# A two-block decoder layer stack in split float32: the second block's products with activations as the stationary operand

## The chip, the cores and the metric

One core of one Trainium2 chip runs the whole program. The metric is the device time of one execution in microseconds (us), lower is better. Engines by the names of the profile: PE is the matrix engine (its weight loads are PEld), DVE the vector engine, ACT the scalar engine, POOL the general one, SP the queue that issues the weight transfers. A matmul on PE holds a block of 128 x 128 numbers in the array (the stationary operand, brought in by a weight load) and streams up to 512 columns past it (the moving operand); the result goes to PSUM, eight banks of 128 x 512 numbers.

## The reference, cut to what matters

256 tokens, 2048 features, all in float32. A first block (a pooling layer and a sparse attention layer, each under a modulated norm) gives `x`; the change is in the second block alone:

```python
def second_block(x, p, ...):
    h = rmsnorm(x, attn_norm_g)
    u, v_sgu, q, k, v_att, g_a, g_b = split(h @ w_in)        # 1024 x 5, 2048 x 2 columns
    ...                                                       # y_a from u, v_sgu; y_b from q, k, v_att
    q, k = rmsnorm(q per head, q_norm_g), rmsnorm(k per head, k_norm_g)      # 8 heads of 128
    merged = sigmoid(g_a) * (y_a @ w_up_a) + sigmoid(g_b) * (y_b @ w_up_b)
    x = x + merged @ w_o
    h = rmsnorm(x, ffn_norm_g)
    gate, up = split(h @ w_ffn_in)                            # 2 x 5632 columns
    x = x + (silu(gate) * up) @ w_ffn_out
    return x + sigmoid(rmsnorm(x, ple_norm_g) @ w_ple_gate) * (p @ w_ple)
```

## The kernel before, in words

Every float32 operand of a large product is split in two numbers of a shorter kind, a high part and a low part (the rest), and a product is three: high x high, high x low, low x high. Weights come from HBM in pieces of 512 rows x 512 columns (1 MB), at most `RAWB = 8` under way. ACT casts half a piece (256 rows) to its high part (`split_half`, L1633), DVE subtracts it to get the low part (`late_low`, L1623); this runs up to `SPLB = 5` half pieces ahead of the products. All of this lies in 20 slots of 8 KB per partition (`F`), handed out by hand, and a slot that a product has read goes to a later split.

A `Group` is a product with 512 columns of a weight, over row tiles of 128 ("row tile" below means 128 rows of one group's 512 columns). `mm_half` (L1690 on) issues it half a piece at a time, and its `orient` says which operand is stationary:

- orient A (weights stationary, features on partitions in the output). Per row tile and each of the four blocks of 128 output features: one matmul of the high weights with the high and low activations side by side (512 columns, L1715) and one of the low weights with the high activations (256 columns, L1719). The output needs four banks, and each bank's two halves are summed in the eviction (`evsum`: ACT copies one, L391, DVE adds, L393).
- orient B (activations stationary, tokens on partitions in the output). Per row tile and each of the two blocks of 128 tokens: three matmuls of 512 columns (L1724 to L1726: high activations with high weights, the same with low weights, low activations with high weights). The output needs two banks.

The order of the work is written out by hand: `seq` lists the pieces, and the loop at the end of the program goes through the halves: splits ahead (`prepare`), products (`mm_half`), and in between it steps generators. Evictions (`evac`, `evq`) are stepped after the products of every output block (`pump_ev`) and after every half; side tasks (`task`, `side`) once per half (`pump`). A generator's `yield` puts off what follows by one step, and `lag(n)` by n; so the place of an eviction's instructions in each engine's queue is set by the number of yields, and the engines run their queues in order. Evictions and tasks share PSUM with the products (from the attention on, `PM` may hold 5 banks and `PA`, the tasks', 3), and small tiles come from slots too (`H` six of 4 KB, `W` three of 2 KB, `E` nine of 1 KB).

Stages, with names of the code: `P1` pool, `P2` attention, `P3` the second block's mixers (groups q0, k0, v0, v1, q1, k1, two of the gating's v, two of its u, then four times g_a, g_b, up_a, up_b, then four of w_o), `P4` the feed-forward part (6 pairs of gate and up groups, four of w_ffn_out over those 6 blocks, then 5 pairs and four more), `P5` the per-layer embedding. Before the change v, the gating's v and P5 are of orient B, the rest of P3 and P4 of orient A. The evictions that matter: `ev_b2qk` and the task `qknorm` (squares on ACT, sums over a head's features by PE with `ones` L1186, the factors spread over partitions by PE L1202, the product on DVE L1205); `ev_sig`, `ev_upa`, `ev_upb`; `ev_residual` (w_o and w_ffn_out); `ev_fgate`, `ev_fup`; `start_b2` (the second block's norm: it makes `Rn` and `En` per token from a PE product, L1118, and then scales the residual in 16 DVE instructions, L1130); `start_ffn` and `start_ple` (norms); `x_natural` (the residual turned to tokens on partitions, 8 times 4 PE transposes, L1468). `split` and `split_scaled` make the operand of the next product from a result with features on partitions.

Of the kernel before, what the change touches and what calls it, by code (L numbers as in the profile page):

```python
# [19 lines left out]
T = 256            # tokens  # L20
# [28 lines left out]
class Slots:  # L49
    """Slots of one size on chip, handed out by hand; the longest free one goes first."""  # L50
# [37 lines left out]
class Share:  # L88
    """A user of slots that others use as well, with no more than cap of them."""
# [19 lines left out]
class Part:  # L109
    """Some of the columns of a slot; the slot is free when all its parts are."""  # L110
# [11 lines left out]
class Op:  # L122
    """An operand with features on partitions: per feature tile the high and low parts, 256 tokens each."""
# [27 lines left out]
class Op32:  # L151
    """An operand with features on partitions, as it is: n feature tiles in a slot."""
# [42 lines left out]
class ModPiece:  # L195
    """Rows and columns of a modulation weight: 128 k x 512 n times (4, 1) or (2, 2)."""
# [12 lines left out]
def model_kernel(ctx: ExitStack, tc: tile.TileContext, A, out):  # L209
# [27 lines left out]
    # ---------------------------------------------------------------- tasks beside the main line of products  # L237
# [38 lines left out]
    def lag(n=2):  # L276
        """Before a product in a task: time for the other engines to get its operands ready."""
# [5 lines left out]
    def last_of(key, n=4):  # L283
        """True for the last of the n output tiles that get here."""
# [6 lines left out]
    def take(where, key, nt, shape=(128, 4, T)):  # L291
        """For the output tiles of a group: its slot, asked for by the first one."""
# [4 lines left out]
    # ---------------------------------------------------------------- constants and small vectors  # L297
# [15 lines left out]
    def rows(i, what):  # L313
        """Vectors as rows of 128, turned into columns."""
# [58 lines left out]

    def split_scaled(op, kt, v, g):
        """v * g (per feature) into operand tile kt."""
# [6 lines left out]
    def evsum(ps, dst=None):  # L382
        """A product in PSUM, its two halves summed if it has two."""
# [16 lines left out]
    class Sum:  # L400
        """Sum of squares over features, per token (still spread over partitions)."""

        def __init__(self, tail=0):
            self.n = self.started = 0
            # the last ones stay apart, for PE to add
# [21 lines left out]
        def total(self, n=3):  # L427
            """Sums per token, on all partitions."""
# [30 lines left out]
    sums = {k: Sum() for k in ("x0", "x2", "x2g", "x3", "x4")}  # L459
# [62 lines left out]
    # ---------------------------------------------------------------- modulation  # L522
# [10 lines left out]
    def mod_work(p, half):  # L533
# [3 lines left out]
        if p.kk + half == 0:  # L537
            # while heads are at work the smaller slots are taken
# [22 lines left out]
    def mod_fin(key, wide, wait):  # L561
        """Sums over partitions, plus the bias; the gain of the norm; the operand that becomes ready."""
# [26 lines left out]
    # ---------------------------------------------------------------- phase 1: pool  # L589
# [4 lines left out]
    def pool_consts():  # L594
        """The pooling over tokens as matrices [s, t], less the identity: tokens 0-127 to all, 128-255 to their own."""
# [124 lines left out]
    # ---------------------------------------------------------------- phase 2: sparse attention  # L720
# [13 lines left out]
    def rope_tables():  # L734
        """cos and signed sin: for heads of 128 (partitions 0-31), of 64 (all partitions), and with
        tokens on partitions for the index keys."""
# [20 lines left out]
        # sign of the sine: minus for the first half of a head's turned features  # L757
# [36 lines left out]
        def reduced(dst, ang, shift):  # L794
            """ang + shift * 2 pi, brought to [-pi, pi]."""
# [37 lines left out]
    # index keys and weights: the last 128 columns (48 of the index queries, 64 keys, 16 weights)  # L833
# [100 lines left out]
    def topk_task():  # L934
        """0 for the keys that a query attends to, a large negative number for the others."""
# [62 lines left out]
    def head_attn(g, j):  # L998
# [25 lines left out]
        # columns: keys 0 of queries 0 and 1, keys 1 of queries 1  # L1024
# [73 lines left out]
    # ---------------------------------------------------------------- phase 3: second block, its mixers  # L1098
# [24 lines left out]
        # eps / R^2, for the norms of q and k  # L1123
# [4 lines left out]
        # the residual that the second block starts from  # L1128
# [6 lines left out]
    def b2_consts():  # L1135
        # stick-breaking looks at strictly earlier keys; partition: key, column: query
# [5 lines left out]
        # [j', j]: 1 where j' >= j  # L1142
# [18 lines left out]
        for g in range(8):  # L1161
            # partition: s, column: t; keep t >= s
# [5 lines left out]
    def ev_b2qk(name, n):  # L1168
        def ev(nt, ps):
            yield from take(blk, (name, n), nt)  # L1170
            yield from evsum(ps, blk[name, n].t[:, nt, :])
            if last_of((name, n)):
                task(qknorm(name, n))
        return ev

    def qknorm(name, n):
        x = blk[name, n].t
        g = vcol("q_norm_g") if name == "q" else kgs
        ss = yield from PA.new([128, 2, 4])
        for j0 in (0, 2):  # L1180
            q = yield from W.new([128, 2, T])
            S.activation(q.t, x[:, j0:j0 + 2, :], AF.Square)
            yield from lag()
            for j in range(2):
                for tt in range(2):
                    PE.matmul(ss.t[:, tt, j0 + j:j0 + j + 1], q.t[:, j, cols(tt)], ones[:, 0:1], start=True, stop=True)  # L1186
            q.free()
        yield from until(lambda: "En" in blk)
        yield
        r = small((128, 2, 4))  # L1190
        V.scalar_tensor_tensor(r, ss.t, 1.0 / 128.0, blk["En"][:, :, None].to_broadcast([128, 2, 4]), op0=ALU.mult,
                               op1=ALU.add)
        ss.free()
        S.activation(r, r, AF.Sqrt)
        V.reciprocal(r, r)
        yield from lag()
        for j0 in (0, 2):
            # each token's factor, on all partitions
# [595 lines left out]
```

## Time and profile before

| | |
|---|---|
| device time, median of 3 runs | 2427.67 us (2427.65 to 2427.88) |
| the profiled execution, first to last instruction (span) | 2425.4 us; no other time of it is given |
| PE busy / weight loads busy | 2382.0 us (98%) / 2089.2 us (86%) |
| DVE / ACT / POOL busy | 1675.9 us (69%) / 1209.2 us (50%) / 121.9 us (5%) |
| matmuls on PE | 13855 |
| DMA | 522.82 MB, mean 216 GB/s |

The profiled execution's own time is known as its span; the median of the runs is 2.3 us more, which is what lies around the first and the last instruction. Busy time of an engine is the union of its instructions' records. Records of matmuls overlap (the next one starts before the record of the one ahead has ended), so a mean duration of a matmul is not its share of the time; the step from one start to the next is read from the timeline. A row of a group of instructions gives line, engine, operation, tiles (written <- read), shapes, count, busy time and mean duration in ns, then the engine's idle time before them and who ended it.

### The profile page before, as it was taken

Reading aid. Unit: us, or ns where it says so; the run is one execution under the profiler, and the core shown is the slowest. Engines: PE = TensorE matmul, PEld = TensorE weight load, DVE = VectorE, ACT = ScalarE, POOL = GpSimd, SP = SyncE. Lnnn points to the kernel's source line nnn. Section 1 sums busy time; section 2 is a strip of 40 time slices with the busy share of each in tenths; the row PEclk is TensorE's granted clock in tenths of the full one; section 3 lists DMA queues with packets and bytes.
Section 4 is the critical chain, followed back from the end, with each engine's and each line's share of the span. In section 5 each row is a group of like instructions: output and inputs, shape, how many; then the busy total and the mean of one; then the engine's idle time right before and its main releaser. Section 6 shows DMA issues by size and latency. Waiting matters only on the chain.

```text
span 2425.4 us, 34213 instructions
## 1 busy us (share of the span) xinstructions
PE 2382.0 (98%) x13855; PEld 2089.2 (86%) x13855; DVE 1675.9 (69%) x2396; ACT 1209.2 (50%) x1777; POOL 121.9 (5%) x218
## 2 busy tenths in 40 slices
PE   5999999999999999999999999999999999999999
PEld 5899998988888888888888888888888888888887
DVE  7987899776978887654575667666565456656564
ACT  3444435444465566454754545555444445445553
POOL 0200084000100000000000000000000000000000
PEclk8999999999999999999999999999999999999999
DMA  9988998845556677444455557455455575456372
GB/s 366 387 299 325 332 341 331 313 157 173 174 187 231 227 276 244 156 139 149 149 187 177 184 168 276 155 195 171 159 185 162 190 248 195 149 181 216 123 244 104
DMA packets 246930, 522.82 MB, mean 216 GB/s; under 512 B 8362, under 2 KB 10644, under 8 KB 246516
## 3 DMA queue, kind: packets, MB, share of 16 engines
q1 hardware_dynamic: 246324, 519.20, 61.9%
q8 instruction: 108, 1.77, 0.3%
q0 software_dynamic: 448, 1.44, 0.2%
q14 instruction: 50, 0.41, 0.0%
HBM read 518.51 MB, written 2.10 MB: 215 GB/s over the span
## 4 chain that ended last, share of the span: by engine, by line
PE 92%; DVE 5%; ACT 1%; issue 1%; DMA 1%; POOL 0%; SPq 0%; DVEq 0%; ACTq 0%; POOLq 0%
PE bank L1715 42%; PE bank L1719 21%; PE bank L1724 5%; PE bank L1726 5%; PE bank L1725 5%; PE bank L1709 3%; PE bank L1712 3%; PE bank L1711 3%; DVE f L1623 2%; DVE h L554 2%; PE bank L1705 1%; PE bank L570 1%; PE bank L472 0%; PE bank L1202 0%; PE bank L639 0%
## 5 line engine op out<-in xcount | busy, mean ns | idle before, releaser
L1715 PE MATMUL bank<-f,f 128*128 128x512 f32 x4432 | 1556.0, 400 | 0.0
L1623 DVE TENSOR_TENSOR f<-f,f 128x1024 fp32r<-128x1024 f32 x788 | 945.9, 1218 | 378.6 <-ACT f L1633 377.9
L1719 PE MATMUL bank<-f,f 128*128 128x256 f32 x4432 | 1196.1, 280 | 0.0
L1633 ACT CAST f<-f 128x1024 fp32r<-128x1024 f32 x788 | 800.3, 1041 | 573.8 <-PE bank L1719 257.7
L1715 PEld LDWEIGHTS bank<-f,f 128*128 128x128 f32 x4432 | 814.0, 188 | 177.0
L1719 PEld LDWEIGHTS bank<-f,f 128*128 128x128 f32 x4432 | 836.3, 189 | 25.7
L393 DVE TENSOR_TENSOR e<-bank,e 128x256 f32<-128x256 f32 x240 | 101.3, 423 | 206.7 <-ACT e L391 205.9
L1709 PE MATMUL bank<-f,f 128*128 128x256 f32 x768 | 221.5, 288 | 0.0
L1711 PE MATMUL bank<-f,f 128*128 128x256 f32 x768 | 218.9, 285 | 0.0
L1712 PE MATMUL bank<-f,f 128*128 128x256 f32 x768 | 218.8, 285 | 0.0
L1724 PE MATMUL bank<-f,f 128*128 128x512 f32 x528 | 211.0, 400 | 4.7 <-ACT f L511 4.7
L391 ACT COPY e<-bank 128x256 f32<-128x256 f32 x281 | 102.7, 370 | 219.2 <-PE bank L1715 217.8
L1726 PE MATMUL bank<-f,f 128*128 128x512 f32 x528 | 207.3, 393 | 1.1 <-DVE f L513 1.1
L1725 PE MATMUL bank<-f,f 128*128 128x512 f32 x528 | 206.7, 391 | 0.0
L554 DVE SCALAR_TENSOR_TENSOR h<-f,csil,h 128x512 f32<-128x512 f32 (+1 forms) x202 | 195.5, 1003 | 2.3 <-DMA f<-in_mod_w_dram 0.5
L1709 PEld LDWEIGHTS bank<-f,f 128*128 128x128 f32 x768 | 149.0, 194 | 2.8 <-issue 2.3
L1711 PEld LDWEIGHTS bank<-f,f 128*128 128x128 f32 x768 | 149.0, 194 | 0.3
L1712 PEld LDWEIGHTS bank<-f,f 128*128 128x128 f32 x768 | 148.9, 194 | 0.0
L1724 PEld LDWEIGHTS bank<-f,f 128*128 128x128 f32 x528 | 100.0, 189 | 27.2 <-ACT f L511 4.8
L1726 PEld LDWEIGHTS bank<-f,f 128*128 128x128 f32 x528 | 99.7, 189 | 24.1 <-DVE f L513 2.3
L1725 PEld LDWEIGHTS bank<-f,f 128*128 128x128 f32 x528 | 100.1, 190 | 19.6
L369 ACT CAST f<-e 128x256 fp32r<-128x256 f32 x100 | 40.4, 406 | 78.4 <-DVE e L1434 29.5
(286 smaller groups left out, 1342.6 us busy)
## 6 DMA issues: line engine op xcount, KB each, us to landing
f<-in_mod_w_dram SPq DMA_DIRECT2D x96, 1024.0 KB, 8.0
f<-in_w_ffn_in_dram SPq DMA_DIRECT2D x88, 1024.0 KB, 5.1
f<-in_attn_w_in_dram SPq DMA_DIRECT2D x72, 1024.0 KB, 5.5
f<-in_w_in_dram SPq DMA_DIRECT2D x72, 1024.0 KB, 5.2
f<-in_w_ffn_out_dram SPq DMA_DIRECT2D x44, 1024.0 KB, 5.1
f<-in_pool_w_in_dram SPq DMA_DIRECT2D x32, 1024.0 KB, 10.3
f<-in_pool_w_out_dram SPq DMA_DIRECT2D x16, 1024.0 KB, 8.2
f<-in_attn_w_out_dram SPq DMA_DIRECT2D x16, 1024.0 KB, 5.5
```

Of the source, the lines that this page charges most:

```text
L391: S.copy(a.t, ps.t[:, T:2 * T])
L554: V.scalar_tensor_tensor(acc, p.slot.t[:, k, :], c, acc, op0=ALU.mult, op1=ALU.add)
L1623: V.tensor_sub(ll, r, hh)
L1633: S.copy(hh[:, :, :nw], r)
L1709: PE.matmul(o, hh[:, i, cols(t)], op.h(kt), start=beg and t % 2 == 0, stop=False, skip_group_check=True)
L1711: PE.matmul(o, hh[:, i, cols(t)], op.l(kt), start=False, stop=False, skip_group_check=True)
L1712: PE.matmul(o, ll[:, i, cols(t)], op.h(kt), start=False, stop=end, skip_group_check=True)
L1715: PE.matmul(b, hh[:, i, cols(t)], op.x(kt), start=beg, stop=end, skip_group_check=True)
L1719: PE.matmul(b[:, 0:T], ll[:, i, cols(t)], op.h(kt), start=False, stop=False, skip_group_check=True)
L1724: PE.matmul(b, xh, hh[:, i, :], start=beg, stop=False, skip_group_check=True)
L1725: PE.matmul(b, xh, ll[:, i, :], start=False, stop=False, skip_group_check=True)
L1726: PE.matmul(b, xl, hh[:, i, :], start=False, stop=end, skip_group_check=True)
```

## The change

Groups q and k (4), g_a and g_b (8), up_a and up_b (8), all of w_ffn_in (22) and w_ffn_out (8) become orient B. Their outputs then have tokens on partitions, so:

- factors per token become per-partition scalars of the activation itself (`ev_sig`, `ev_fgate`, `ev_fup`), and evictions read PSUM directly, 512 columns at a time, without `evsum`;
- what is the operand of a next product is turned back to features on partitions by PE transposes, four of 128 x 128 per 512 columns and token block: new helper `turned` (for `merged` and `act`), in `ev_b2qk` (for q and k), and `h4_task` (for the last gate's operand);
- the norm of q and k is done per token on ACT and DVE (`qknorm` with its PE products is gone);
- the residual is turned to tokens on partitions at the start of the feed-forward part (in `start_ffn`; `x_natural` at its end is gone), w_ffn_out adds to that (`ev_ffn_out`), and the last norm's sums of squares come from ACT's accumulator instead of DVE and PE.

The groups of w_o and of the gating's u stay orient A. Comments are removed too, so line numbers of the changed file differ.

```diff
+TL = 3
...
+    def turned(op, b, tt, a):
+        yield from lag(TL)
+        ps = yield from PA.new([128, 4, 128])
+        for j in range(4):
+            PE.transpose(ps.t[:, j, :], a.t[:, cols(j)], ident)
+        a.free()
+        yield
+        yield from op.room(4 * b)
+        op.x(4 * b)
+        t = op.s[b].t
+        hi, lo = t[:, :, cols(tt)], t[:, :, T + tt * 128:T + tt * 128 + 128]
+        S.copy(hi, ps.t)
+        yield
+        V.tensor_sub(lo, ps.t, hi.bitcast(F32))
+        ps.free()
+        if last_of((id(op), b), 2):
+            op.done.update(range(4 * b, 4 * b + 4))
...
     def ev_b2qk(name, n):
...
+        def ev(tt, ps):
+            yield from take(blk, (name, n), tt)
+            a = yield from W.new()
+            S.activation(a.t, ps.t, AF.Square)
+            yield from until(lambda: "En" in blk)
+            yield
+            r = small((128, 4))
+            V.tensor_reduce(r, heads(a.t), axis=AX.X, op=ALU.add)
+            V.tensor_scalar(r, r, 1.0 / 128.0, blk["En"][:, tt:tt + 1], op0=ALU.mult, op1=ALU.add)
+            yield
+            S.activation(r, r, AF.Sqrt)
+            yield
+            V.reciprocal(r, r)
+            V.tensor_mul(heads(a.t), heads(ps.t), r[:, :, None].to_broadcast([128, 4, 128]))
+            ps.free()
+            yield from lag(TL)
+            ps = yield from PA.new([128, 4, 128])
+            for j in range(4):
+                PE.transpose(ps.t[:, j, :], a.t[:, cols(j)], ident)
+            a.free()
+            yield
+            S.activation(blk[name, n].t[:, :, cols(tt)], ps.t, AF.Identity, scale=g)
...
-    def qknorm(name, n):
...
     def ev_sig(name):
-            a = yield from evsum(ps)
-            V.tensor_mul(a.t, a.t, blk["R"].t)
-            yield
-            S.activation(blk[name].t[:, nt, :], a.t, AF.Sigmoid)
+            S.activation(blk[name].t[:, tt, :], ps.t, AF.Sigmoid, scale=blk["Rn"][:, tt:tt + 1])
...
     def ev_upb(n):
+            a = yield from W.new()
+            V.tensor_mul(a.t, ps.t, blk["gb"].t[:, tt, :])
+            ps.free()
+            V.tensor_add(a.t, a.t, blk["ga"].t[:, tt, :])
...
+            yield from turned(merged, n, tt, a)
...
     def start_ffn():
...
+        ps = yield from PA.new([128, 2])
+        for tt in range(2):
+            PE.matmul(ps.t[:, tt:tt + 1], s.s.t[:, cols(tt)], ones[:, 0:1], start=True, stop=True)
...
+        for n in range(4):
+            for tt in range(2):
+                ps = yield from PA.new()
+                for j in range(4):
+                    PE.transpose(ps.t[:, cols(j)], xt(n * 4 + j)[:, cols(tt)], ident)
+                yield
+                S.copy(ple["x"][tt].t[:, cols(n, 512)], ps.t)
...
     def ev_fup(g):
+            a = yield from W.new()
+            V.scalar_tensor_tensor(a.t, ps.t, ffn["R"][:, tt:tt + 1], ffn["g"].t[:, tt, :], op0=ALU.mult, op1=ALU.mult)
+            ps.free()
...
+            yield from turned(act, g, tt, a)
...
+    def ev_ffn_out(n, last):
+        def ev(tt, ps):
+            yield from until(lambda: ple["xn"] > n)
+            x = ple["x"][tt].t[:, cols(n, 512)]
+            V.tensor_add(x, ps.t, x)
+            ps.free()
+            if last:
+                yield
+                q = yield from W.new()
+                S.activation(q.t, x, AF.Square, accum_out=ssq[:, tt, n:n + 1])
...
+    def h4_task(n):
+        yield from lag(TL)
+        for k in (0, 2):
+            ps = yield from PA.new([128, 2, T])
+            for j in range(2):
+                for tt in range(2):
+                    PE.transpose(ps.t[:, j, cols(tt)], ple["x"][tt].t[:, cols(n * 4 + k + j)], ident)
+            evac(h4_split(n * 4 + k, ps))
+            yield
...
-        P3.append(Group(W_in2, n0, h2, ALLK, ev_b2qk(name, n),
+        P3.append(Group(W_in2, n0, h2, ALLK, ev_b2qk(name, n), orient="B",
...
-            P4.append(Group(W_fi, HID + g * 512, h3, ALLK, ev_fup(g), fin=h3.free if g == 10 else None))
+            P4.append(Group(W_fi, HID + g * 512, h3, ALLK, ev_fup(g), orient="B", fin=h3.free if g == 10 else None))
...
-            P4.append(Group(W_fo, n * 512, act, range(c0, c1), ev_residual(n, h4 if lastc else None, "ple_norm_g", "x4"),
-                            fin=fin if n == 3 else None))
+            P4.append(Group(W_fo, n * 512, act, range(c0, c1), ev_ffn_out(n, lastc), orient="B",
+                            pre=(lambda: preload(AF.Sqrt)) if lastc and n == 3 else None, fin=fin if n == 3 else None))
```

Three places of the two programs' instruction lists follow; in them lines of the old program are those of the profile, and of the new one L1138 is the old L1118 (the product that gives `Rn`), L1176 the old L1156 (constants), L1664 the old L1623 (low parts of weights), L1150 the old L1130, L1765 to L1767 the old L1724 to L1726; L1213 and L380 are transposes, and the new L1202 is the sum over a head on DVE. A line of "..." leaves out rows of matmuls that only continue a bank.

PE at the start of P3, before: q0 and k0 are of orient A, and the norm's small products stand between the matmuls of v0 (`bank_252`, `bank_253`).

```order
L1118 MATMUL bank_251_9158<-ident_69,e_168_9083 128x1 x2
...
L1156 MATMUL bank_256_9283<-ident_69,h_47_8853 128x128 x4
L1202 MATMUL bank_257_9288<-ident_69,small_9228 128x128 x4
L1724 MATMUL bank_252_9235<-f_590_9161,f_538_8335 128x512
...
L1202 MATMUL bank_258_9318<-ident_69,small_9228 128x128 x4
L1186 MATMUL bank_255_9258<-ones_70,w_63_9259 128x1 x4
```

The same place now (`bank_243` and `bank_244` are k0's, `bank_247` and `bank_250` v0's, `w_61` to `w_63` the normed q0 and k0).

```order
L1138 MATMUL bank_246_9093<-ident_69,e_164_9042 128x1 x2
L1765 MATMUL bank_243_8974<-f_585_9025,f_564_8772 128x512
...
L1765 MATMUL bank_247_9129<-f_587_9044,f_524_8119 128x512
...
L1176 MATMUL bank_248_9149<-ident_69,h_47_8843 128x128 x4
L1176 MATMUL bank_249_9162<-ident_69,h_47_8843 128x128 x4
L1765 MATMUL bank_250_9186<-f_587_9044,f_524_8119 128x512
...
L1765 MATMUL bank_247_9129<-f_588_9061,f_524_8119 128x512
...
L1213 MATMUL bank_251_9202<-ident_69,w_63_9105 128x128 x4
L1213 MATMUL bank_252_9207<-ident_69,w_62_8966 128x128 x4
L1213 MATMUL bank_253_9212<-ident_69,w_61_8958 128x128 x4
```

Between the product for `Rn` and the first transposes of q and k stand 30 matmuls of 512 columns (12 of k0, 18 of v0) and 8 transposes of constants; three batches of transposes then follow each other.

DVE at the same place now, from the copy of `Rn` to the last of the three products that those transposes read.

```order
L1141 COPY Rn_9116<-bank_246_9093 128x2
...
L1150 SCALAR_TENSOR_TENSOR f_3_102<-f_3_102,cols_5_76,e_162_8931 128x256 x4
L1664 TENSOR_TENSOR f_593_9126<-f_577_8929,f_593_9126 128x1024
L1202 TENSOR_REDUCE small_9136<-w_63_9105 128x4
...
L1150 SCALAR_TENSOR_TENSOR f_3_102<-f_3_102,cols_5_76,e_162_8931 128x256 x4
L1150 SCALAR_TENSOR_TENSOR f_4_103<-f_4_103,cols_5_76,e_162_8931 128x256 x4
L1207 RECIPROCAL small_9136<-small_9136 128x4
L1208 TENSOR_TENSOR w_63_9105<-bank_243_8974,small_9136 128x512
...
L1208 TENSOR_TENSOR w_61_8958<-bank_240_8794,small_9142 128x512
```

Twelve of the sixteen scalings of the residual, one subtraction for the weights, three sums over heads and the three products stand ahead of the last batch.

DVE where the first up group of P4 ends, before (four banks, `bank_406` to `bank_409`; L393 sums a bank's halves, L1432 and L1434 are the factors, L371 the low part for the next product).

```order
L1623 TENSOR_TENSOR f_918_14285<-f_899_14013,f_918_14285 128x1024
L393 TENSOR_TENSOR e_298_14310<-bank_406_14161,e_298_14310 128x256
L393 TENSOR_TENSOR e_299_14317<-bank_407_14168,e_299_14317 128x256
L1432 TENSOR_TENSOR e_298_14310<-e_298_14310,e_293_14076 128x256
L393 TENSOR_TENSOR e_300_14325<-bank_408_14174,e_300_14325 128x256
...
L1434 TENSOR_TENSOR e_298_14310<-e_298_14310,h_71_14125 128x256
L1623 TENSOR_TENSOR f_919_14304<-f_899_14013,f_919_14304 128x1024
...
L371 TENSOR_TENSOR f_921_14342<-e_298_14310,f_921_14342 128x256
```

DVE where an up group ends now (`bank_384` and `bank_385` hold it; L389 is the low part, from the transposes' banks).

```order
L1664 TENSOR_TENSOR f_944_13712<-f_931_13577,f_944_13712 128x1024
L1463 SCALAR_TENSOR_TENSOR w_79_13735<-bank_384_13617,R_88_13220,h_72_13602 128x512
L1463 SCALAR_TENSOR_TENSOR w_80_13743<-bank_385_13624,R_88_13220,h_72_13602 128x512
L1664 TENSOR_TENSOR f_945_13727<-f_931_13577,f_945_13727 128x1024
L1664 TENSOR_TENSOR f_947_13748<-f_934_13612,f_947_13748 128x1024
L389 TENSOR_TENSOR f_948_13775<-bank_387_13758,f_948_13775 128x4x128
```

PE at the same place now (`bank_386` and `bank_388` are the next group's).

```order
L1767 MATMUL bank_384_13617<-f_939_13663,f_892_13099 128x512
L1765 MATMUL bank_385_13624<-f_939_13663,f_892_13099 128x512
...
L1765 MATMUL bank_386_13751<-f_941_13680,f_856_12503 128x512
...
L380 MATMUL bank_387_13758<-ident_69,w_79_13735 128x128 x4
L1765 MATMUL bank_388_13763<-f_941_13680,f_856_12503 128x512
```

One DVE instruction per token block stands where there were sixteen per group, and the transposes of a token block stand 12 matmuls of 512 columns behind the last matmul of its bank.

## Rows read from the trace of the kernel before

**Rows 1.** The page: busy time by engine, granted clock in 40 slices.

```profile
PE 2382.0 (98%) x13855; PEld 2089.2 (86%) x13855; DVE 1675.9 (69%) x2396; ACT 1209.2 (50%) x1777; POOL 121.9 (5%) x218
PEclk8999999999999999999999999999999999999999
```

**Rows 2.** Waits of PE from 915 us to the end: total, times, longest.

```profile
PE bank L1262 <- ACT h L1257: 0.9, 1, 0.9
```

**Rows 3.** Groups of instructions by shape, PE: orient A, the norm's products, transposes.

```profile
L1715 PE MATMUL bank<-f,f 128*128 128x512 f32 x4432 | 1556.0, 400 | 0.0
L1719 PE MATMUL bank<-f,f 128*128 128x256 f32 x4432 | 1196.1, 280 | 0.0
L1202 PE MATMUL bank<-ident,small 128*128 128x128 f32 x64 | 8.4, 274 | 0.0
L1186 PE MATMUL bank<-ones,w 128*128 128x1 f32 x64 | 7.6, 239 | 0.0
L1468 PE MATMUL bank<-ident,f 128*128 128x128 f32 x32 | 4.8, 272 | 0.0
```

**Rows 4.** Timeline of PE in P4, orient A: start, record, engine, line.

```profile
1699.84 0.40 PE L1715 MATMUL bank<-f,f 128*128 128x512 f32 x1
1700.07 0.28 PE L1719 MATMUL bank<-f,f 128*128 128x256 f32 x1
...
1705.49 0.40 PE L1715 MATMUL bank<-f,f 128*128 128x512 f32 x1
```

**Rows 5.** Timeline of PE in P5, orient B.

```profile
2345.01 0.39 PE L1726 MATMUL bank<-f,f 128*128 128x512 f32 x1
2345.24 0.39 PE L1724 MATMUL bank<-f,f 128*128 128x512 f32 x1
...
2351.81 0.39 PE L1726 MATMUL bank<-f,f 128*128 128x512 f32 x1
```

**Rows 6.** Windows: stretch, PE, PEld, DVE, ACT, POOL busy (count), granted clock, DMA share, GB/s.

```profile
1640.00:1840.00 200.00, 200.00 (x1136) 173.61 (x1135) 120.67 (x175) 97.63 (x141) 0.00 (x0) 1.00 0.52 169
2340.00:2380.00 40.00, 40.00 (x178) 33.11 (x177) 24.86 (x27) 19.25 (x21) 0.00 (x0) 1.00 0.53 180
```

**Rows 7.** Timeline of PE in P5: orient B, and one batch of four transposes in it.

```profile
2332.22 0.40 PE L1725 MATMUL bank<-f,f 128*128 128x512 f32 x1
...
2334.53 0.39 PE L1726 MATMUL bank<-f,f 128*128 128x512 f32 x1
2334.77 0.60 PE L1468 MATMUL bank<-ident,f 128*128 128x128 f32 x4
...
2335.43 0.40 PE L1725 MATMUL bank<-f,f 128*128 128x512 f32 x1
```

**Rows 8.** Timeline of PE in P3: one batch of the norm's small products.

```profile
1024.44 0.39 PE L1726 MATMUL bank<-f,f 128*128 128x512 f32 x1
1024.67 1.05 PE L1202 MATMUL bank<-ident,small 128*128 128x128 f32 x8
...
1025.79 0.39 PE L1725 MATMUL bank<-f,f 128*128 128x512 f32 x1
```

**Rows 9.** Timeline at the start of P3: PE's product for Rn, then DVE.

```profile
992.28 0.50 PE L1118 MATMUL bank<-ident,e 128*128 128x1 f32 x4
...
992.82 0.16 DVE L1121 COPY Rn<-bank 128x2 f32<-128x2 f32 x1 [1.71 <-PE bank L1118]
993.49 1.67 DVE L1130 SCALAR_TENSOR_TENSOR f<-f,cols,e 128x256 f32<-128x256 f32 x4
```

**Rows 10.** Groups by shape, DVE and ACT, from 915 us to the end: prices of evictions.

```profile
L1623 DVE TENSOR_TENSOR f<-f,f 128x1024 fp32r<-128x1024 f32 x517 | 622.6, 1222 | 338.6 <-ACT f L1633 338.1
L1518 DVE TENSOR_TENSOR w<-w,h 128x512 f32<-128x512 f32 x8 | 5.5, 689 | 32.1 <-ACT w L1515 32.1
L1294 DVE TENSOR_REDUCE sguss<-h 128x8 f32<-128x1024 f32 x2 | 2.4, 1212 | 0.0
```

**Rows 11.** Timeline of DVE around the end of an up group in P4.

```profile
1706.80 0.42 DVE L393 TENSOR_TENSOR e<-bank,e 128x256 f32<-128x256 f32 x1 [4.45 <-ACT e L391]
```

More of the change, by code (lines that the diff above doesn't have):

```diff
@@ L457, in xt @@
         return res[kt // 8].t[:, kt % 8, :]
-    sums = {k: Sum() for k in ("x0", "x2", "x2g", "x3", "x4")}
+    sums = {k: Sum() for k in ("x0", "x2", "x2g", "x3")}
     sums["x1"] = Sum(TAIL)
@@ L1168, in ev_b2qk @@
     def ev_b2qk(name, n):
[L1169 to L1173, printed above, removed]
-        return ev
-    def qknorm(name, n):
[L1177 to L1188, printed above, removed]
-        yield
[L1190 to L1197, printed above, removed]
-            ps = yield from PA.new([128, 2, T])
-            for j in range(2):
-                for tt in range(2):
-                    PE.matmul(ps.t[:, j, cols(tt)], r[:, tt, j0 + j:j0 + j + 1].to_broadcast([128, 128]), ident,
-                              start=True, stop=True)
-            yield
-            V.scalar_tensor_tensor(x[:, j0:j0 + 2, :], x[:, j0:j0 + 2, :], g, ps.t, op0=ALU.mult, op1=ALU.mult)
-            ps.free()
-        yield from lag()
-        blk["normed", name, n] = True
@@ new lines, in ev_b2qk, with heads @@
+        g = vcol("q_norm_g") if name == "q" else kgs
+        def heads(t):
+            return t.rearrange("p (h d) -> p h d", h=4)
+        def ev(tt, ps):
[21 more added lines that the diff above has]
+            ps.free()
+            yield from lag()
+            if last_of((name, n), 2):
+                blk["normed", name, n] = True
@@ L1413, in model_kernel @@
     ffn = {}
+    ple = {"xn": 0}
     def start_ffn():
-        ps = yield from sums["x3"].total()
-        blk["R"].free()
-        ffn["R"] = yield from rstd(ps)
-    def ev_fgate(nt, ps):
-        yield from take(ffn, "g", nt)
-        a = yield from evsum(ps)
-        yield from until(lambda: "R" in ffn)
-        V.tensor_mul(a.t, a.t, ffn["R"].t)
-        yield
-        S.activation(ffn["g"].t[:, nt, :], a.t, AF.Silu)
-        a.free()
-    def ev_fup(g):
-        def ev(nt, ps):
-            a = yield from evsum(ps)
-            V.tensor_mul(a.t, a.t, ffn["R"].t)
-            yield
-            V.tensor_mul(a.t, a.t, ffn["g"].t[:, nt, :])
-            yield
-            yield from split(act, g * 4 + nt, a.t)
-            a.free()
-            if last_of("fup"):
-                ffn.pop("g").free()
-        return ev
+        s = sums["x3"]
+        yield from until(lambda: s.n == KT)
+        yield from lag()
+        ps = yield from PA.new([128, 2])
+        for tt in range(2):
+            PE.matmul(ps.t[:, tt:tt + 1], s.s.t[:, cols(tt)], ones[:, 0:1], start=True, stop=True)
+        s.s.free()
+        blk["R"].free()
+        yield
+        r = tl(const, [128, 2], "R3")
+        S.activation(r, ps.t, AF.Sqrt, scale=1.0 / D, bias=epsc)
+        ps.free()
+        yield
+        V.reciprocal(r, r)
+        ffn["R"] = r
+        yield from F.room(2)
+        ple["x"] = [F.get() for _ in range(2)]
+        for n in range(4):
[3 more added lines that the diff above has]
+                    PE.transpose(ps.t[:, cols(j)], xt(n * 4 + j)[:, cols(tt)], ident)
+                yield
+                S.copy(ple["x"][tt].t[:, cols(n, 512)], ps.t)
+                ps.free()
+            ple["xn"] += 1
+            if n % 2:
+                res[n // 2].free()
@@ new lines, in h4_task, with h4_split @@
+    def h4_task(n):
[6 more added lines that the diff above has]
+            evac(h4_split(n * 4 + k, ps))
+            yield
+    def h4_split(kt, ps):
+        yield
+        for j in range(2):
+            yield from split_scaled(h4, kt + j, ps.t[:, j, :], vcol("ple_norm_g", kt + j, 1))
+        ps.free()
@@ L1451, in fin @@
                     act.free(b)
-            P4.append(Group(W_fo, n * 512, act, range(c0, c1), ev_residual(n, h4 if lastc else None, "ple_norm_g", "x4"),
-                            fin=fin if n == 3 else None))
+            P4.append(Group(W_fo, n * 512, act, range(c0, c1), ev_ffn_out(n, lastc), orient="B",
+                            pre=(lambda: preload(AF.Sqrt)) if lastc and n == 3 else None, fin=fin if n == 3 else None))
     pT = Op(F)
-    ple = {"xn": 0}
-    def x_natural(n):
-        yield from lag(3)
-        if n == 0:
-            yield from F.room(2)
-            ple["x"] = [F.get() for _ in range(2)]
-        yield from until(lambda: "x" in ple)
-        for tt in range(2):
-            ps = yield from PA.new()
-            for j in range(4):
-                PE.transpose(ps.t[:, cols(j)], xt(n * 4 + j)[:, cols(tt)], ident)
-            yield
-            S.copy(ple["x"][tt].t[:, cols(n, 512)], ps.t)
-            ps.free()
-        ple["xn"] += 1
     def p_task():
@@ L1488, in start_ple @@
     def start_ple():
-        s = sums["x4"]
-        yield from until(lambda: s.n == KT)
-        yield from lag()
-        ps = yield from PA.new([128, 2])
-        for tt in range(2):
-            PE.matmul(ps.t[:, tt:tt + 1], s.s.t[:, cols(tt)], ones[:, 0:1], start=True, stop=True)
-        s.s.free()
+        r = tl(const, [128, 2], "Rp")
         yield
-        r = tl(const, [128, 2], "Rp")
-        S.activation(r, ps.t, AF.Sqrt, scale=1.0 / D, bias=epsc)
-        ps.free()
+        V.tensor_reduce(r, ssq, axis=AX.X, op=ALU.add)
+        yield
+        S.activation(r, r, AF.Sqrt, scale=1.0 / D, bias=epsc)
         yield
@@ L1512, in ev @@
         def ev(tt, ps):
-            yield from until(lambda: "R" in ple and ple["xn"] > n)
+            yield from until(lambda: "R" in ple)
             s = yield from W.new()
@@ L1527, in model_kernel @@
     for n in range(4):
-        P5.append(Group(A["w_ple_2"][0], n * 512, pT, [0], ev_ple(n), orient="B", nk=2,
-                        pre=(lambda: task(start_ple())) if n == 0 else None))
+        P5.append(Group(A["w_ple_2"][0], n * 512, pT, [0], ev_ple(n), orient="B", nk=2))
         P5.append(Group(A["w_ple_gate_2"][0], n * 512, h4, ALLK, ev_pgate(n), orient="B"))
```

57 lines of the change are left out of this document (33 added, 24 removed).

## The prediction

> **What bounds the kernel now.** I read the page first, then PE's waits, then the stages' windows and timelines. PE is busy for 98% of the span, and its granted clock stands at the upper of its two levels, 2.4 GHz, from the second fortieth on [rows 1]. From 915 us, where the second block starts, to the end, PE waits for others 0.9 us in all [rows 2]. In a stretch of the feed-forward part PE is full, DVE has 120.67 of 200 us, ACT 97.63, DMA a share of 0.52 [rows 6]. So in the stages that the change touches the time is the sum of PE's steps, and faster evictions are worth nothing by themselves. What counts: how long PE needs for the same products in the other orient, what PE work comes in and goes, and whether PE is made to wait.
>
> **The trap in the durations.** The records of matmuls are 400 ns (512 columns) and 280 ns (256) [rows 3]. Added up they give 4 x 680 = 2720 ns for a row tile of orient A, and about 6 x 395 = 2370 ns for orient B. But the records overlap: starts follow each other by 0.23 and 0.12 us [rows 4]. I use steps from start to start alone.
>
> **What each part costs on PE.**
>
> Orient A: 16 pairs of a 512-column and a 256-column matmul take 1705.49 - 1699.84 = 5.65 us, 0.353 us a pair [rows 4]; 1136 instructions in 200 us give 0.352 [rows 6]. A row tile has four pairs: 1.410 us. Orient B: 30 matmuls take 2351.81 - 2345.01 = 6.80 us, 0.2267 each [rows 5]; the window of 40 us with 178 agrees to 1%, as its count takes in those cut at the edges [rows 6]. A row tile has six: 1.360 us. Both have 3072 columns per row tile; B has six matmuls and weight loads, A eight.
>
> Row tiles that change: q and k 4 x 16 = 64, g_a and g_b 8 x 16 = 128, up_a and up_b 8 x 8 = 64, w_ffn_in 22 x 16 = 352, w_ffn_out 4 x 44 = 176; 784 of the 4432 / 4 = 1108 of orient A [rows 3]. Saved: 784 x 0.050 = **39.2 us**.
>
> Transposes added: 8 batches of four for q and k, 8 for `merged`, 22 for `act`, 8 for the last gate's operand: 46. The residual's 8 batches only move from the end of the feed-forward part to its start. One batch between matmuls of orient B: from 2334.53 to 2335.43 there are 0.90 us for two matmuls and the batch, so 0.90 - 0.45 = 0.445 us [rows 7]. Added: 46 x 0.445 = **20.5 us**.
>
> Gone: the small products of `qknorm`, 64 instructions at L1202 and 64 at L1186 [rows 3], 16 batches of eight. One costs 1025.79 - 1024.44 - 2 x 0.227 = 0.90 us [rows 8]; I price the L1186 batches alike. Removed: **14.4 us**. The small products of the two later norms come out even within half a microsecond.
>
> Added waits. (1) The start of P3, the place shown in the lists. The norm of q0 and k0 must wait for `En`. Counted from the start of the product for `Rn`, DVE's copy comes at 0.54 us and the first four scalings end at 2.9 [rows 9]. Then come a subtraction (1.22) [rows 10] that needs its cast, so 4.1 to 4.6; three sums over 512 columns, half of the 1212 ns row with a small instruction behind, 0.8 each [rows 10]; eight scalings at 0.42 [rows 9]; and three products at 689 ns with a small reciprocal, 0.85 each [rows 10]. The first product is there at about 10.7, the third at 12.4. PE has 30 matmuls, two batches of transposes and the product itself ahead: 6.8 + 0.9 + 0.4 = 8.1 us. It reaches the first of the three batches at 8.1 and leaves the third about 4 us later than it could. I take **4 us**, ends 0 (splits run five halves ahead, nothing starves) and 8 (the casts wait too). (2) For q1 and k1 the same chain has no scalings in it and no wait for `En`; PE arrives later than the products: 0. (3) The last up_b is followed by w_o in orient A, with only four matmuls per output block between eviction steps: the two products of 0.69 us per token block are late by up to 0.5 us twice: **1 us**. (4) An up group of the feed-forward part: the transposes stand 12 matmuls behind, 2.7 us; DVE has one instruction of about 0.7 us to do there and was idle 4.45 us before such a group's end [rows 11]: 0.
>
> What costs nothing: the evictions (DVE and ACT get less work, and are off the path); the residual's early turn (two more slots for some 25 us, while only one block of `act` is there); two banks instead of four per group (PE waits for no bank now); weights that come 4% faster than at a DMA share of 0.52 [rows 6]; the end of the program, where P5 is as before.
>
> **Sum.** -39.2 + 20.5 - 14.4 + 4 + 1 = -28.1 us. The profiled execution, 2425.4 us from first to last instruction, becomes 2397.3; the median of the runs is 2.3 us over that span, so 2427.7 becomes **2399.6 us**.
>
> **A rule that speaks against it.** On the matmul's fixed part rows 4 and 5 say 0.2267 us for 512 columns, and 0.353 us for 768 in two matmuls; two matmuls fewer per row tile are worth 50 ns. The Trainium skill's page "TensorE: Matmul & The Clock Gate", section "Back-to-back issue gap", gives the isolated step as N / 2.4 + 2.5 ns. By it A would take 1300 and B 1295 ns per row tile, the saving would be an estimated 4 us, and the sum 2435. The trace disagrees: its steps are longer than that by 11 to 14 ns per matmul.
>
> **Rivals.**
>
> *PE waits for its transposes* (slower). A batch in program order stops everything behind it until DVE has made its input. The gain is gone when the 30 batches behind up_b and the up groups wait 28.1 / 30 = 0.94 us each. One subtraction of the weight splits standing in front each time (1.22 us [rows 10]) gives 36.6 us: 2436. For it: DVE runs in order and has 60% of the stage [rows 6]. Against: it is idle ahead of a group's end [rows 11], and 2.7 us are given. 6 in 100.
>
> *A transpose costs its record.* The record is 272 ns [rows 3], 184 of them 50.0 us in place of 20.5: 2429, no change. Where a batch starts late because of its input, its four cannot overlap what is ahead. Against: in rows 7 four take 0.35 us together to the next start. 4 in 100. The same page of the Trainium skill, section "Part 4: PE-mode transpose", gives about 275 ns for one in a kernel; the record agrees, the step here is a third of it.
>
> *The step of orient B is longer where DVE and ACT are at work.* Ten steps in P5 took 2334.53 - 2332.22 = 2.31 us, 0.231 each [rows 7]. At that, a row tile takes 1.386 us, the saving is 18.8 us, the time 2420: still faster. 7 in 100.
>
> *The records are right after all*: 2720 - 2370 = 350 ns per row tile, 274 us, about 2165. Rows 4 against rows 3 say no; 1 in 100.
>
> **How the numbers follow.** My case has 80 in 100; another 2 go to something that makes it nothing. Faster by over 0.2% (4.9 us, about what a measurement of this kernel can tell from no change): 80 + 7 + 1 = 88. Within: 4 + 2 = 6. Slower: 6. The range: at the low end no added wait and 0.052 us per row tile (0.353 x 4 against 1.360), -40.8 + 20.5 - 14.4 = -34.7, 2393, and 2 us for the steps' rounding: 2391. At the high end 0.043 us per row tile, as the step of B lies between 0.2267 and 0.231 (-33.7), with 8 us at P3's start, the 1 us and a quarter of a microsecond in each of the 22 batches of `act` (5.5): -33.7 + 20.5 - 14.4 + 14.5 = -13.1, rounded to 2415.
>
> **What would show it.** In the profile after: PE's steps of 0.227 us at the three lines of orient B throughout the feed-forward part, with PE still at 98%; 4 x 324 = 1296 matmuls left at each of the two lines of orient A; one wait of PE on DVE of some 3 to 5 us some 10 us into P3 and little else from 915 us on; batches of transposes at 0.44 us; DVE's busy time lower without any effect. I am wrong if the step in P4 is over 0.229, if PE's waits on DVE from 915 us on add up to over 10 us, or if the weights come late (waits of ACT on DMA).

## The result, and the profile after

The changed kernel takes 2401.16 us (median of 4 runs, 2400.56 to 2402.44), the kernel before on the same chip 2427.66 us (4 runs). The ratio is 0.9892, 95% interval 0.9878 to 0.9906: 26.5 us faster. Forecast were 2399.6 us, 28.1 us faster. The profiled execution took 2400.56 us, its span is 2398.9 us against 2425.4. So 1.7 us lie around the span here, and not the 2.3 that the forecast added; the other 0.6 was the spread between executions of the kernel before.

The page of the changed kernel, busy time by engine and the granted clock in 40 slices, the lines that answer to [rows 1]:

```profile
PE 2353.2 (98%) x12341; PEld 2017.6 (84%) x12341; DVE 1560.0 (65%) x1986; ACT 1138.5 (47%) x1522; POOL 119.9 (5%) x218
PEclk8999999999999999999999999999999999999999
```

PE is as full as it was, with 1514 matmuls and weight loads fewer. DVE lost 116 us of work and ACT 71; the time lost 26.5. The groups of instructions by shape, PE, of the changed kernel (L1765 to L1767 are orient B, L1756 and L1760 orient A, L380 the transposes of `turned`, L1213 those of q and k), to be read beside [rows 3]:

```profile
L1765 PE MATMUL bank<-f,f 128*128 128x512 f32 x2096 | 828.1, 395 | 4.7 <-ACT f L531 4.7
L1756 PE MATMUL bank<-f,f 128*128 128x512 f32 x1296 | 460.4, 402 | 0.0
L1760 PE MATMUL bank<-f,f 128*128 128x256 f32 x1296 | 349.9, 280 | 0.0
L380 PE MATMUL bank<-ident,w 128*128 128x128 f32 x120 | 18.0, 272 | 0.0
L1213 PE MATMUL bank<-ident,w 128*128 128x128 f32 x32 | 5.8, 330 | 3.3 <-DVE small L1207 3.3
```

1296 matmuls are left at each of the two lines of orient A, and 1568 came to each line of orient B (2096 - 528, two for each of 784 row tiles). The means of the records are what they were; they tell nothing of the gain. The steps do. Timeline of PE in the feed-forward part of the changed kernel (start, record, engine, line), to be read beside [rows 4, 5]:

```profile
1640.18 0.39 PE L1766 MATMUL bank<-f,f 128*128 128x512 f32 x1
1640.41 0.39 PE L1767 MATMUL bank<-f,f 128*128 128x512 f32 x1
...
1646.98 0.39 PE L1766 MATMUL bank<-f,f 128*128 128x512 f32 x1
...
1740.92 0.39 PE L1767 MATMUL bank<-f,f 128*128 128x512 f32 x1
1741.16 0.60 PE L380 MATMUL bank<-ident,w 128*128 128x128 f32 x4
...
1741.83 0.40 PE L1766 MATMUL bank<-f,f 128*128 128x512 f32 x1
```

Thirty steps take 6.80 us, 0.2267 each, the same number as in P5 before. A batch of four transposes costs 1741.83 - 1740.92 less two steps: 0.91 - 0.45 = 0.46 us.

PE's waits from 915 us to the end in the changed kernel (engine, line, releaser: total, times, longest), to be read beside [rows 2], and the place of the one wait on PE and DVE:

```profile
PE bank L1213 <- DVE small L1207: 3.3, 1, 3.3
```

```profile
999.98 0.39 PE L1767 MATMUL bank<-f,f 128*128 128x512 f32 x1
1003.66 2.79 PE L1213 MATMUL bank<-ident,w 128*128 128x128 f32 x12 [3.29 <-DVE small L1207]
1006.10 0.78 PE L1765 MATMUL bank<-f,f 128*128 128x512 f32 x1
```

```profile
992.51 0.16 DVE L1141 COPY Rn<-bank 128x2 f32<-128x2 f32 x1 [2.33 <-PE bank L1138]
...
999.28 3.41 DVE L1150 SCALAR_TENSOR_TENSOR f<-f,cols,e 128x256 f32<-128x256 f32 x8
1002.62 0.17 DVE L1207 RECIPROCAL small<-small 128x4 f32<-128x4 f32 x1
1002.82 0.69 DVE L1208 TENSOR_TENSOR w<-bank,small 128x512 f32<-128x512 f32 x1
...
1004.44 0.69 DVE L1208 TENSOR_TENSOR w<-bank,small 128x512 f32<-128x512 f32 x1
```

This is the wait that the prediction placed: PE stands before the first transposes of q0 and k0 while DVE scales the residual. From 999.98 to 1006.10 there are 6.12 us. One step (0.23) and twelve transposes at 0.105 us (E3 below), 1.3 us, would be due: about 4.6 us are lost, where the waits view counts 3.3. The rest is no further wait. Windows around the place (stretch, PE, PEld, DVE, ACT, POOL busy and counts, granted clock, DMA share, GB/s):

```profile
1000.00:1003.00 3.00, 0.37 (x2) 0.00 (x0) 2.97 (x9) 1.52 (x3) 2.83 (x7) 1.00 0.00 0
1004.00:1006.00 2.00, 2.00 (x11) 1.97 (x10) 1.97 (x6) 1.17 (x3) 0.00 (x0) 0.50 0.01 4
1007.00:1010.00 3.00, 3.00 (x15) 2.45 (x14) 2.88 (x5) 2.26 (x4) 0.00 (x0) 1.00 0.25 43
```

PE works without a gap from 1004 to 1006 us, but after it had stood for 3.3 us its granted clock is 0.50, the lower of its two levels (1.2 GHz). The twelve transposes take 2.44 us, 0.203 each. By 1007 us the clock is back at 1.00. How much the clock alone cost can only be estimated: the third product ends at 1005.13, and four transposes at 0.105 us behind it would end at 1005.55 in place of 1006.10, so about 0.5 us of the 4.6; the rest would have been waits between the batches.

### The profile page after: what moved, and what is told of

It is laid out like the page before. It is cut to its first block, busy times and chain, and to the rows that moved or that the text cites. A ratio compares the mean times of both kernels' runs of the same rounds, so it can differ in the third digit from the quotient of the medians.

```text
span 2398.9 us, 30505 instructions
## 1 busy us (share of the span) xinstructions
PE 2353.2 (98%) x12341; PEld 2017.6 (84%) x12341; DVE 1560.0 (65%) x1986; ACT 1138.5 (47%) x1522; POOL 119.9 (5%) x218
## 4 chain that ended last, share of the span: by engine, by line
PE 64%; DVE 2%; ACT 1%; DMA 0%; issue 0%; ACTq 0%
PE bank L1767 17%; PE bank L1765 17%; PE bank L1766 17%; PE bank L1756 6%; PE bank L1760 3%; DVE f L1664 1%; PE bank L380 1%; ACT f L1674 0%; DMA f<-in_attn_w_in_dram 0%; DVE f L574 0%; PE bank L1213 0%; DMA f<-in_attn_w_out_dram 0%; PE bank L1338 0%; PE bank L1446 0%; PE bank L1495 0%
## 5 line engine op out<-in xcount | busy, mean ns | idle before, releaser
L1664 DVE TENSOR_TENSOR f<-f,f 128x1024 fp32r<-128x1024 f32 x788 | 943.6, 1219 | 517.8 <-ACT f L1674 517.4
L1765 PE MATMUL bank<-f,f 128*128 128x512 f32 x2096 | 828.1, 395 | 4.7 <-ACT f L531 4.7
L1767 PE MATMUL bank<-f,f 128*128 128x512 f32 x2096 | 818.4, 390 | 1.1 <-DVE f L533 1.1
L1766 PE MATMUL bank<-f,f 128*128 128x512 f32 x2096 | 817.3, 390 | 0.0
L1765 PEld LDWEIGHTS bank<-f,f 128*128 128x128 f32 x2096 | 394.7, 188 | 86.5 <-ACT f L531 4.8
L1767 PEld LDWEIGHTS bank<-f,f 128*128 128x128 f32 x2096 | 394.1, 188 | 85.6 <-DVE f L533 2.3
L1766 PEld LDWEIGHTS bank<-f,f 128*128 128x128 f32 x2096 | 394.8, 188 | 79.8
L1756 PE MATMUL bank<-f,f 128*128 128x512 f32 x1296 | 460.4, 402 | 0.0
L1760 PE MATMUL bank<-f,f 128*128 128x256 f32 x1296 | 349.9, 280 | 0.0
L1756 PEld LDWEIGHTS bank<-f,f 128*128 128x128 f32 x1296 | 238.6, 188 | 50.9
L1760 PEld LDWEIGHTS bank<-f,f 128*128 128x128 f32 x1296 | 244.6, 189 | 7.7
L1750 PE MATMUL bank<-f,f 128*128 128x256 f32 x768 | 221.5, 288 | 0.0
L1752 PE MATMUL bank<-f,f 128*128 128x256 f32 x768 | 218.9, 285 | 0.0
L1753 PE MATMUL bank<-f,f 128*128 128x256 f32 x768 | 218.8, 285 | 0.0
L1750 PEld LDWEIGHTS bank<-f,f 128*128 128x128 f32 x768 | 148.9, 194 | 2.7 <-issue 2.3
L1752 PEld LDWEIGHTS bank<-f,f 128*128 128x128 f32 x768 | 148.9, 194 | 0.3
L1753 PEld LDWEIGHTS bank<-f,f 128*128 128x128 f32 x768 | 148.8, 194 | 0.0
L411 ACT COPY e<-bank 128x256 f32<-128x256 f32 x81 | 29.3, 370 | 66.4 <-PE bank L1756 66.4
L413 DVE TENSOR_TENSOR e<-bank,e 128x256 f32<-128x256 f32 x56 | 23.6, 422 | 53.8 <-ACT e L411 53.7
L1463 DVE SCALAR_TENSOR_TENSOR w<-bank,R,h 128x512 f32<-128x512 f32 x22 | 16.5, 751 | 53.7 <-PE bank L1767 53.7
```

The lines of the kernel that those rows point to most:

```text
L411: S.copy(a.t, ps.t[:, T:2 * T])
L1664: V.tensor_sub(ll, r, hh)
L1750: PE.matmul(o, hh[:, i, cols(t)], op.h(kt), start=beg and t % 2 == 0, stop=False, skip_group_check=True)
L1752: PE.matmul(o, hh[:, i, cols(t)], op.l(kt), start=False, stop=False, skip_group_check=True)
L1753: PE.matmul(o, ll[:, i, cols(t)], op.h(kt), start=False, stop=end, skip_group_check=True)
L1756: PE.matmul(b, hh[:, i, cols(t)], op.x(kt), start=beg, stop=end, skip_group_check=True)
```

## The experiments

Each was timed beside the kernel before on one chip; its median there was 2427.14 us in the first four, 2427.43 in the last three. The interval of each ratio is some 3 us wide to each side, so differences of a microsecond between two experiments are not shown by their times alone. "Against the change" below is the 26.5 us of the change less each kernel's own gain over the kernel before.

**E1: q and k as before.** The eviction and `qknorm` of before, orient A, all else changed.

```diff
-        P3.append(Group(W_in2, n0, h2, ALLK, ev_b2qk(name, n), orient="B",
+        P3.append(Group(W_in2, n0, h2, ALLK, ev_b2qk(name, n),
```

> The changed kernel with q and k as before (orient A, the norm by small PE products); everything else changed. Theory (PE's steps are the time): 64 row tiles x 0.050 us more (3.2), 8 batches of transposes less (-3.6), 16 batches of small products back (14.4), the wait of PE at the start of P3 gone (3.3 us in the waits, about 4.7 by the steps there): +9.3 us, 2410.5 us. Rival (only the orient of the big products counts, small ones hide in the array's gaps): +3.2 us less the wait, about 2400. PE's wait on DVE at P3's start should be under 1 us in both.

Measured: 2409.83 us, ratio 0.9927 (0.9914 to 0.9939), 17.3 us faster than before, so 9.2 us of the change are q and k's. PE's waits from 915 us on in E1:

```profile
PE bank L1282 <- ACT h L1277: 0.9, 1, 0.9
```

The wait at L1213 is gone with its cause, and the old one of [rows 2] is back. The granted clock at that place is 1.00 (1004.5 to 1006 us), as it is in E7, while E2, E3 and E5, which have the wait, show 0.50 to 0.63 there. The rival, by which the small products hide, is out by 10 us: a third of the change's gain came with q and k, where by the terms of the sum the orient itself is worth less than its transposes (3.2 against 3.6 us) and the 128 small instructions that left PE are the rest. The price of these instructions holds for both kinds: a batch with one column (L1186) takes 1016.69 - 1015.33 less two steps, 0.91 us, where [rows 8] has 0.90 for 128 columns. Timeline of PE in P3 of the kernel before:

```profile
1015.33 0.39 PE L1726 MATMUL bank<-f,f 128*128 128x512 f32 x1
1015.56 0.95 PE L1186 MATMUL bank<-ones,w 128*128 128x1 f32 x8
...
1016.69 0.40 PE L1725 MATMUL bank<-f,f 128*128 128x512 f32 x1
```

**E2: g_a, g_b, up_a, up_b as before.**

```diff
-        P3.append(Group(W_in2, 5120 + n * 512, h2, ALLK, ev_sig("ga"), orient="B"))
+        P3.append(Group(W_in2, 5120 + n * 512, h2, ALLK, ev_sig("ga")))
...
-        P3.append(Group(A["w_up_b_2"][0], n * 512, yb, range(2), ev_upb(n), orient="B", fin=yb.free if end else None))
+        P3.append(Group(A["w_up_b_2"][0], n * 512, yb, range(2), ev_upb(n), fin=yb.free if end else None))
```

> The changed kernel with g_a, g_b, up_a and up_b as before (orient A), the rest changed. Theory: 192 row tiles x 0.050 us more (9.6), 8 batches of transposes less (-3.6): +6.0 us, 2407.2 us. Rival (the evictions that got lighter are what was won): DVE and ACT do more again but PE is not made to wait, so this rival would need waits of PE on DVE or ACT in the mixers of over 2 us, which the theory has at none.

Measured: 2406.89 us, ratio 0.9914 (0.99 to 0.9927), 20.3 us faster than before; these groups are worth 6.2 us. The only wait of PE there is the one at P3's start:

```profile
PE bank L1213 <- DVE small L1207: 3.3, 1, 3.3
```

So the heavier evictions make nothing wait, and what the groups are worth fits PE's own steps less the transposes (6.0 expected).

**E3: each batch of `turned` done twice.**

```diff
-        for j in range(4):
-            PE.transpose(ps.t[:, j, :], a.t[:, cols(j)], ident)
+        for _ in range(2):
+            for j in range(4):
+                PE.transpose(ps.t[:, j, :], a.t[:, cols(j)], ident)
```

> The changed kernel with each of the 30 batches of transposes behind up_b and the up groups done twice (same result). Theory (a batch costs its steps): 30 x 4 x 0.108 us = 13.0 us more, 2414 us. Rival (a transpose costs its record of 272 ns): 120 x 0.272 = 32.6 us more, 2434 us. A third: they hide, 2401 us.

Measured: 2413.19 us, ratio 0.9941 (0.9929 to 0.9954), 12.5 us above the change for 120 transposes: 0.105 us each (0.08 to 0.13 within the interval of E3). By their records it would have been 32.6. The span says the same, 2411.5 against 2398.9. They don't hide, and they don't cost their records.

**E4: the residual's scalings put off.**

```diff
+        yield from lag(6)
         for kt in range(KT):
             V.scalar_tensor_tensor(xt(kt), xt(kt), vcol("final_g", kt, 1), r1.t, op0=ALU.mult, op1=ALU.mult)
```

> The changed kernel with the 16 scalings of the residual put off by six steps of the side tasks, so that DVE has the norm of q0 and k0 first. Theory (PE waits at the first transposes of q and k because 12 scalings, 5.1 us of DVE, stand ahead of the products): the wait of 3.3 us and the slack between the three batches go, -3.5 to -4.5 us, 2397 us. Rival (the chain through the sums and ACT's roots sets it, or weights' casts): the wait stays over 2 us and the time at 2400 to 2401.

Measured: 2397.32 us, ratio 0.9875 (0.9861 to 0.9888), 29.8 us faster than before and 3.3 us faster than the change; its interval and the change's overlap, but the runs don't (2396.30 to 2398.13 against 2400.56 to 2402.44, beside kernels before that differ by half a microsecond). PE's waits, PE at the place of the wait, and the window around it (columns as above), in E4:

```profile
PE bank L1214 <- DVE w L1209: 0.2, 1, 0.2
```

```profile
1001.26 1.38 PE L1214 MATMUL bank<-ident,w 128*128 128x128 f32 x8
1002.79 0.66 PE L1214 MATMUL bank<-ident,w 128*128 128x128 f32 x4 [0.15 <-DVE w L1209]
```

```profile
1000.00:1007.00 7.00, 6.76 (x35) 5.09 (x34) 5.94 (x13) 6.33 (x11) 2.99 (x8) 1.00 0.15 37
```

The sums, the roots and the weights' subtraction are still in the queue, so it was the scalings. With the wait the stretch at the lower clock is gone too, and the 3.3 us hold both. This version is faster than both kernels.

**E5: no steps between the eviction and the transposes.**

```diff
     def turned(op, b, tt, a):
-        yield from lag(TL)
+        yield from lag(0)
```

> The changed kernel with the transposes behind up_b and the up groups issued at once, no steps between the eviction and them (q and k as they are). It gives the rival 'PE waits for its transposes' its conditions. Theory: PE then waits for DVE in each batch, about 0.9 us for an up group's one instruction (0.7 us and the signals) and 1.6 us for up_b's two: 22 x 0.9 + 8 x 1.6 = 33 us more, about 2434 us, slower than the kernel before. If the place did not matter (PE's queue slack takes it up), 2401 us.

Measured: 2438.29 us, ratio 1.0042 (1.0029 to 1.0056): 10.9 us slower than the kernel before, 37.4 above the change. PE's waits in E5, and one of its batches in the feed-forward part:

```profile
PE bank L380 <- DVE w L1463: 18.6, 22, 0.8
PE bank L380 <- DVE w L1376: 12.3, 8, 1.6
PE bank L1213 <- DVE small L1207: 3.3, 1, 3.3
```

```profile
1664.81 0.39 PE L1767 MATMUL bank<-f,f 128*128 128x512 f32 x1
1666.05 0.66 PE L380 MATMUL bank<-ident,w 128*128 128x128 f32 x4 [0.84 <-DVE w L1463]
...
1666.77 0.39 PE L1766 MATMUL bank<-f,f 128*128 128x512 f32 x1
```

All 30 batches wait. 1666.77 - 1664.81 less two steps is 1.51 us for a batch that costs 0.46 when its input is there: 1.05 us more, of which the view shows 0.84. When its input is there, a batch starts before the record of the matmul ahead has ended (1741.16 against 1740.92 + 0.39 in the changed kernel above); a batch that waits loses this overlap, 0.15 of the other 0.2 us. So the rival "PE waits for its transposes" has the mechanism and the size it was given; three steps of the program's order are what keeps it away.

**E6: the feed-forward part of the kernel before in twelve matmuls of 256 columns.**

```diff
-            P4.append(Group(W_fi, HID + g * 512, h3, ALLK, ev_fup(g), fin=h3.free if g == 10 else None))
+            P4.append(Group(W_fi, HID + g * 512, h3, ALLK, ev_fup(g), orient="A3", fin=h3.free if g == 10 else None))
```

The same for the gate groups and for w_ffn_out.

> The kernel before with all of the feed-forward part in the third orient that it has (weights stationary as in orient A, but three matmuls of 256 columns per block: twelve per row tile). Same layout of the output as orient A, no transposes, lighter evictions. Theory (a matmul has a fixed share of 13 to 16 ns and the columns cost the same): 1.440 against 1.410 us, 528 row tiles x 0.030 = 15.8 us more than before, 2443 us. Rival (the gain of orient B is in which operand is stationary or in the evictions, not in the number of matmuls): no slower than before, 2427 us or less.

Measured: 2443.15 us, ratio 1.0064 (1.0049 to 1.0079), 15.7 us slower than before. Timeline of PE in E6:

```profile
1699.89 0.28 PE L1711 MATMUL bank<-f,f 128*128 128x256 f32 x1
1700.02 0.28 PE L1712 MATMUL bank<-f,f 128*128 128x256 f32 x1
...
1705.30 0.28 PE L1711 MATMUL bank<-f,f 128*128 128x256 f32 x1
```

45 steps in 5.41 us are 0.1202 each. If a step has a fixed part and a part per column, the same in both orients, the 0.2267 for 512 columns leave 0.1065 us for 256 columns and 14 ns for a matmul whatever its columns. Evictions are lighter in this form, the weights are still stationary and no transpose was added, and still it is slower, so the rival is out: from twelve matmuls a row tile (1.442 us) to six (1.360), each one left out is worth 14 ns.

Two things stay open. Orient A, with eight, does not lie on that line: by it, four matmuls more would have cost 55 ns a row tile, 29 us in all, where 30 ns and 15.7 us came; the last section returns to this. And E6 does not tell a matmul from its weight load. The window of its feed-forward part shows the records of the loads without a gap, 200.00 of 200 us against 173.61 in [rows 6], so the 0.1202 may be set by the loads:

```profile
1640.00:1840.00 200.00, 200.00 (x1669) 200.00 (x1668) 105.76 (x137) 92.39 (x141) 0.00 (x0) 1.00 0.49 167
```

**E7: the feed-forward part alone changed** (E1 and E2 together).

> The changed kernel with both q, k and the merge groups as before, so that the feed-forward part alone is changed. Theory (the parts add up): 528 x 0.050 = 26.4 us saved, 30 batches of transposes (22 for act, 8 for the last gate) 13.4 us, so 13.0 us faster than before, 2414 us. If the parts interact (slots, DVE's queue), it differs from that by more than 2 us.

Measured: 2415.53 us, ratio 0.9949 (0.9936 to 0.9961), 11.9 us faster than before. With the 9.2 of E1 and the 6.2 of E2 that is 27.3 where the change has 26.5: the parts add up within what the runs can tell.

## Why the prediction was right, point by point

- **PE's steps bound the time.** Right: 116 us less work for DVE moved nothing, E2 put some of it back without a wait, and the parts of E1, E2 and E7 add up to the whole.
- **The saving per row tile, 0.050 us.** Right in kind, perhaps a little too large. The step of orient B was met to the digit (0.2267), so the rival with 0.231 is out. E7 gives (11.9 + 13.4) / 528 = 0.048 us, E2 (6.2 + 3.6) / 192 = 0.051, with batches at 0.445; their intervals (0.006 and 0.016) cannot tell 0.048 from 0.050. The window of [rows 6], 0.352 us a pair, gives 1.408 against 1.360 and so 0.048; the short stretch of [rows 4] gave the larger end. At 0.048 the term is 37.6 us in place of 39.2. With the terms below as measured (4.6 for the wait, none at up_b) the sum is -26.9 where -26.5 was measured; that it comes so near is partly luck, as the measured interval is 3 us to each side.
- **The transposes, 0.445 us a batch.** Right: 0.46 in the row above, and 0.105 us per transpose in E3. Both rivals on it are out, that of the record by 20 us.
- **The small products of q and k, 14.4 us.** Right: E1 measures 9.2 us for q and k together, and the batches at L1186, priced alike without a row of their own, took 0.91 us. The terms were 3.2 saved, 3.6 for transposes, 14.4 removed and 4 of added wait: 10.0; with the 4.6 us measured for the wait, 9.4.
- **The wait at the start of P3, 4 us.** Right in place and cause: E4 got 3.3 us back by moving the scalings alone. The size, 4.6 us by the steps, holds a part that the prediction had no term for: the granted clock fell to 0.50 after the wait, about 0.5 us by the estimate above.
- **The wait at the last up_b, 1 us.** Wrong, by 1 us: the waits view has none there.
- **The slower rival** did not come, as the cover that the prediction counted (12 matmuls, 2.7 us, against one DVE instruction) was there. E5 took the cover away, and the change was then slower than the kernel before.
- **The rule on the matmul's fixed part.** By the Trainium skill's page "TensorE: Matmul & The Clock Gate", section "Back-to-back issue gap", it would be 2.5 ns for the isolated step. E6 and the rows above give 14 ns per matmul in this stream, each with its own weight load. Whether the weight load causes the rest was not tried.

## What to carry to other kernels

Where PE is full, price a change by the steps from one start to the next, not by records: at the same number of columns, each of the two matmuls left out per row tile was worth 24 ns, and a float32 transpose of 128 columns cost 0.105 us. Turning 512 columns of 256 tokens back takes two batches, 0.9 us, and that is what about 19 row tiles save (0.9 / 0.048, an estimate). So q and k, with 16 row tiles for each 512 columns turned back, gave all of it back, the operand of w_ffn_out, with 32 (gate and up), a little over half. Small products that only spread or sum a norm's factors cost PE 0.9 us per batch of eight whatever DVE and ACT do meanwhile, so where DVE and ACT have room, move them there. The one wait of PE of 3.3 us cost more than its length, as the granted clock was at 0.50 behind it. And put a transpose far enough behind its input in program order: three steps were the difference between 26 us faster and 11 us slower.

## What the runs showed of the hardware that had not been expected

A pair of matmuls of orient A takes 0.352 to 0.353 us [rows 4, 6], while the step of 512 columns among its like (0.2267) and that of 256 columns among its like (0.1202, E6) add up to 0.347. So the mixed order costs 5 to 6 ns a pair more than its parts, some 22 ns of the 48 that a row tile gained. Why, is open: no run here has the two widths in another order, or one weight load for two matmuls.

The wait of 3.3 us at the start of P3 left PE at a granted clock of 0.50 (1004 to 1006 us), where transposes took 0.203 us each in place of 0.105. From 915 to 2390 us it is the only place where the changed kernel's clock falls, and E4, without the wait, has 1.00 there.
